# Fused 512-column products for the input projections of a two-layer hybrid decoder

## The chip, the cores and the metric

The kernel runs on one core of one Trainium2 chip. The metric is the device time of one execution in microseconds (us). TensorE is called PE here (its weight loads PEld), VectorE DVE, ScalarE ACT, GpSimd POOL, and SyncE SP; SP issues the loads.

## The reference

Two layers work on one sequence of 256 positions and 2048 features, in fp32. Each layer is `x + RMSNorm_post(mixer(RMSNorm_pre(x)))`.

```python
# layer 0
u = h @ w_in                                # 2048 -> 8192
xr, zr, xm, zm = jnp.split(u, [LRU_WIDTH, 2 * LRU_WIDTH, 2 * LRU_WIDTH + MLSTM_WIDTH], axis=-1)
xr = causal_dwconv(xr, lru_conv_w, lru_conv_b);  yr = rg_lru(xr, ...)
xmc = silu(causal_dwconv(xm, ...));  ym = mlstm_chunkwise(q, k, v, ig, fg) ...
y = concat([yr * silu(zr), ym * silu(zm)]);  return y @ w_out
# layer 1
u = h @ w_in                                # 2048 -> 16384
rkv, z = u[..., :3 * RWKV_WIDTH], u[..., 3 * RWKV_WIDTH:]
rkv = rkv + (shift_right(rkv) - rkv) * mu_rkv;  r, k, v = jnp.split(rkv, 3, axis=-1)
y = rwkv7_scan(rh, wh, kh, vh, kk, ah) ...  ;  return (y * silu(z)) @ w_out
```

`rwkv7_scan` is a recurrence over positions with a 64x64 state for each of 64 heads. The kernel computes it in four chunks of 64 positions, which needs the inverse of a triangular 64x64 matrix for each chunk and head.

## The kernel before

**Precision.** An fp32 product is made of three products of rounded parts. A weight piece `raw` is split into a high part `whi` (a cast on ACT) and a low part `wlo` = raw - whi (a subtraction on DVE), by `split_w`. The normalised input h, features on partitions, positions on columns, is split likewise into `hh` and `hl`. The sum whi x hh + whi x hl + wlo x hh goes to PSUM.

**The input projections** are made by `in_proj`, 512 output features at a time: 16 calls in layer 0 and 32 in layer 1. Layer 1 has eight groups of 512 features (8 heads), each with four calls, in the order k, r, z, v. A call takes 8 pieces, each 256 input features by 512 output features: 512 KB by one DMA of SP, 4 KB in a row, into one of four `raw` buffers (`RAW_BUFS`; three each of `whi` and `wlo`). A piece is 24 matmuls of 256 columns (`in_mms`): 8 of whi x hh alternating with 8 of whi x hl, on the same weights, then 8 of wlo x hh. Two PSUM banks (`gb`, from a pool of four) collect the call's result, and the consumers read it there: the convolutions `conv`, the token shift `shifted` (two operations for each quarter, on ACT and DVE) and the gate `silu2`. For xm, ACT first copies it to SBUF.

**What sets the order.** PE's program order is the order in which matmuls are written (`InOrder` chains them). All other work, such as the recurrences, is written by generators that `Weave` advances: `wv_.tick(dt)` after every few projection matmuls adds dt us to a planned clock, and a generator whose due time has come writes its next step there. DVE and ACT are ordered by a scheduler that ranks instructions by the place where they were written, with `split_w` moved ahead (`high_priority(offset=AHEAD)`). Once built, each engine's order is fixed, and an engine that waits for one instruction holds all those behind it.

**One group of layer 1**, by the names that follow. `keys` forms BK and AR from k. `blocks` has PE multiply them (`mb<-AR,BK 64x64`), and DVE writes the result to `Aab`. `inverse` transposes that to `Ab` and runs 31 dependent steps on DVE (`tf<-Ab,Tb`, then `Tb<-Tb,tf`), then transposes to `TT` and `ZT`; PE then multiplies `ZT,Aab` and `TT,ZT`. In between, `scores` needs the half of `AR` that DVE makes from r (`AR<-rt,Pe`) and has PE multiply `AR,BK 64x128`. `recur` walks the four chunks, each a chain from PE to ACT (`Ws`), PE, DVE (`UV`, two halves of 64 partitions) and PE (`UV,BKt`), while the next group's keys are made. `vt<-gb,vec,vt` is the shift of v, `bi<-Rc,BK` belongs to the value path, `th` to the decay of the next group.

The input tiles of a layer, four of 4 x 128 features, are made on demand by the generator `tiles`, between the first pieces of the layer's first call.

Of the kernel before, what the change touches and what calls it, by code (L numbers as in the profile page):

```python
# [7 lines left out]
F32 = mybir.dt.float32  # L8
F32R = mybir.dt.float32r
# [4 lines left out]
P = 128  # L14
T = 256
# [129 lines left out]
def two_layers(ctx, tc, x, gpost, cst, selc, v0, v1, w_in0, w_out0, w_in1, w_out1, lruw, qkvw,  # L145
# [17 lines left out]
    def gbank():  # L163
        return pg.tile([P, 512], F32, name="gb", tag="gb")

    def mbank():
        return pm.tile([P, 512], F32, name="mb", tag="mb")
# [53 lines left out]
    def in_mms(banks, hi, lo, pc, h, nft, tick):  # L221

        def mm(part, kk, f, hx, first=False, last=False):
            pe.matmul(banks[f // 2][:, (f % 2) * T:(f % 2 + 1) * T], lhsT=part[:, kk, f * P:(f + 1) * P], rhs=hx,
                      start=first, stop=last, skip_group_check=True)

        hs = [tuple(t[:, (2 * pc + kk) % 4, :] for t in h[(2 * pc + kk) // 4]) for kk in range(2)]
# [24 lines left out]
    def half(banks, f):  # L252
        return banks[f // 2][:, (f % 2) * T:(f % 2 + 1) * T]

    def split_y(src, yl):
        yh = hp.tile([P, 4, T], F32R, name="yh", tag="hp")
        act.copy(yh, src)
        dve.tensor_tensor(yl, src, yh.bitcast(F32), SUB)
        return yh, yl

    def out_proj(wsrc, get_y, evac, tick, finish, after, room=None):


# [12 lines left out]
        def piece(c, pc, banks):
            hi, lo = weights(c, pc)
            for part in range(3):
                for kk in range(2):
                    for tt in range(2):  # L280
                        mm(c, pc, hi, lo, part, kk, tt, banks[tt])
                    wv_.tick(tick)

        pair = [[gbank(), gbank()] for _ in range(2)]
        for c in range(2):
            for pc in range(14):
                piece(c, pc, pair[c])
        wv_.drain()
        finish()
        for c in range(2):  # L290
            for pc in range(14, 16):
                piece(c, pc, pair[c])
            evac(c, pair[c])
        for c in range(2, 4):
            banks = [gbank(), gbank()]
# [38 lines left out]
    def to_features(xs, dg, g, warm):  # L334


        banks = {}

        def turn(c, tt):
            if c not in banks:  # L340
                banks[c] = [mbank(), mbank()]
            for f2 in range(2):
                for f in range(2):
                    pe.matmul(banks[c][f2][:, f * T + tt * P:f * T + (tt + 1) * P], lhsT=xs[c][:, tt, (2 * f2 + f) * P:(2 * f2 + f + 1) * P],
                              rhs=dg[tt], start=(tt == 0 and f == 0), stop=True, skip_group_check=True)

        h = []

        def tiles():
            banks[2] = [gbank(), gbank()]  # L350
            keep_warm(warm[0], banks[2][0])
            for c in range(2):
                turn(c, 0)
            keep_warm(warm[1], banks[2][0])
            turn(2, 0)
            for c in range(4):
                if c == 3:
                    turn(c, 0)
                turn(c, 1)
                hh = hp.tile([P, 4, T], F32R, name="hh", tag="hp")  # L360
                hl = hp.tile([P, 4, T], F32R, name="hl", tag="hp")
                for i in range(4):
                    bf = half(banks[c], i)
                    activ(hh[:, i, :], bf, AF.Copy, scale=g(4 * c + i))
                    dve.scalar_tensor_tensor(hl[:, i, :], bf, g(4 * c + i), hh[:, i, :].bitcast(F32), MUL, SUB)
                h.append((hh, hl))
                yield

        grow[0] = tiles()
        next(grow[0])  # L370
        return h
# [20 lines left out]
    def silu2(banks, sz):  # L392

        for b in range(2):
            bk = banks[b].rearrange("p (a t) -> p a t", a=2)
# [24 lines left out]
    with ExitStack() as l0:  # L420
# [230 lines left out]
        def lru(c, yc, lw, res):  # L651
# [24 lines left out]
                                   yc.rearrange("p a t -> p (a t)"), 0.0, MUL, ADD)  # L676
            yield 2.4

        prev = None
        for c in range(4):  # L680
            banks = in_proj(w_in0[(8 + c) * 8:(9 + c) * 8], h)
            wv_.drain(prev)
            xm = t4("xm")
            for b in range(2):
                act.copy(xm[:, 2 * b:2 * b + 2, :], banks[b].rearrange("p (a t) -> p a t", a=2))
            prev = wv_.add(mlstm_in(c, xm))
        wv_.add(gates())
        y0, heads = [], []
        for c in range(4):
            lw = t4("lw")  # L690
            nc.sync.dma_start(lw.rearrange("p a t -> p (a t)"), lruw[:, c, :])
            banks = in_proj(w_in0[c * 8:(c + 1) * 8], h)
            if c == 0:
                wv_.drain(prev)
            yc = t4("yc")
# [6 lines left out]
            banks = in_proj(w_in0[(4 + c) * 8:(5 + c) * 8], h)  # L702
            wv_.drain(g1_)
            sz = t4("sz")
            silu2(banks, sz)
# [1 line left out]
            dve.scalar_tensor_tensor(y, yc, 0.25, sz, MUL, MUL)  # L707
            y0.append(y)
        for c in range(4):
            banks = in_proj(w_in0[(12 + c) * 8:(13 + c) * 8], h)  # L710
            wv_.drain(heads[c])
            sz = t4("sz")
            silu2(banks, sz)
# [28 lines left out]
    with ExitStack() as l1:  # L742
# [38 lines left out]

        def loras():

            banks = [gbank(), gbank()]
# [373 lines left out]
        sts = [{} for _ in range(NG)]  # L1158
        for g in range(NG):
            st = sts[g]  # L1160
            banks = in_proj(w_in1[(8 + g) * 8:(9 + g) * 8], h)
            if g:
                wv_.drain(val[g - 1])
            st["k"] = gt("kt", "kr")
# [20 lines left out]
            banks = in_proj(w_in1[(16 + g) * 8:(17 + g) * 8], h)  # L1185
# [116 lines left out]
```

## Time and profile before

| | |
|---|---|
| time, median of 3 runs | 1917.0 us (1916.63 to 1918.4) |
| the profiled execution | 1918.1 us, span 1916.3 us |
| granted PE clock, mean | 0.995 |
| PE busy | 1890.5 us, 99% |
| DVE busy | 1394.7 us, 73% |
| ACT busy | 1045.2 us, 55% |
| load queue q1 | 45.0% of 16 engines' span |

Lines of a group read: line, engine, operation, output <- inputs, shape, count | busy us, mean ns of one | idle time just before them and what ended it. Lines of the timeline read: start, length, engine, line, operation, with idle time ahead in brackets. L117 and L133 are the lines of the helpers that issue PE's and the other engines' instructions, so tiles tell them apart, not lines. Matmuls overlap, and their mean durations exceed the distance of their starts.

### The profile page before, as it was taken

The page shows a single profiled execution, that of the slowest core. Times are in us where ns is not written, and L with a number is a line of the kernel's source. Part 1 is how long each engine was busy: PE and PEld are TensorE (multiplying, and loading weights), DVE is VectorE, ACT ScalarE, POOL GpSimd, SP SyncE. Part 2 cuts the span into 40 slices and gives each one's busy share as a digit, 9 for nine tenths or more (in the row PEclk, how much of TensorE's full clock was granted, in tenths as well). Part 3 has the DMA queues.
Part 4 walks back from the last instruction along what each step waited for, and adds up shares of the span by engine and source line. Part 5 has one row for each costly group of instructions (what it writes and reads, how often), then busy time and mean ns, then how long its engine had stood idle before and what let it go on. Part 6 is the DMA issues. An engine that isn't in the chain of part 4 may idle for free.

```text
span 1916.3 us, 39538 instructions
## 1 busy us (share of the span) xinstructions
PE 1890.5 (99%) x16506; PEld 1753.2 (91%) x16507; DVE 1394.7 (73%) x2302; ACT 1045.2 (55%) x1609; POOL 59.1 (3%) x84
## 2 busy tenths in 40 slices
PE   9999999999999999999999999999999999999998
PEld 8999999999888899989999999999999999997886
DVE  5667777767555679879689689597796896895544
ACT  6445666645444546555565555655655655555442
POOL 0000000000000000000000000000000000000000
PEclk9999999999999999999999999999999999999999
DMA  7333544445666444423434334344343433356654
GB/s 254 138 133 111 176 165 171 152 173 197 214 202 202 165 144 147 155 106 137 143 130 143 123 130 157 109 150 146 116 147 133 141 133 133 122 186 201 211 202 156
DMA packets 86947, 299.63 MB, mean 156 GB/s; under 512 B 9576, under 2 KB 12392, under 8 KB 86768
## 3 DMA queue, kind: packets, MB, share of 16 engines
q1 hardware_dynamic: 86768, 297.11, 45.0%
q8 instruction: 129, 2.11, 0.4%
q14 instruction: 50, 0.41, 0.1%
HBM read 289.20 MB, written 7.86 MB: 155 GB/s over the span
## 4 chain that ended last, share of the span: by engine, by line
PE 93%; DVE 4%; ACT 1%; issue 1%; DMA 1%; POOL 0%; SPq 0%; DVEq 0%; POOLq 0%; ACTq 0%
PE gb L117 75%; PE mb L117 17%; DVE wlo L133 2%; PE mb L120 1%; ACT whi L133 1%; DVE wb L133 1%; DMA raw<-in_w_in_dram 0%; DVE rt L133 0%; DVE Tb L133 0%; DMA xq<-in_x_dram 0%; DVE tf L133 0%; DVE Ab L133 0%; DVE yT L133 0%; ACT ZT L133 0%; ACT vt L133 0%
## 5 line engine op out<-in xcount | busy, mean ns | idle before, releaser
L133 DVE TENSOR_TENSOR wlo<-raw,whi 128x1024 fp32r<-128x1024 f32 x509 | 619.6, 1218 | 344.2 <-ACT whi L133 308.4
L133 ACT CAST whi<-raw 128x1024 fp32r<-128x1024 f32 x509 | 532.3, 1048 | 553.4 <-PE gb L117 505.1
L117 PE MATMUL gb<-hh,whi 128*128 128x256 f32 x3120 | 793.5, 290 | 2.9 <-ACT whi L133 2.9
L117 PE MATMUL gb<-hl,whi 128*128 128x256 f32 x3120 | 773.7, 284 | 0.5 <-DVE hl L133 0.5
L117 PEld LDWEIGHTS gb<-hh,whi 128*128 128x128 f32 x3120 | 598.8, 192 | 13.6 <-ACT whi L133 3.7
L117 PEld LDWEIGHTS gb<-hl,whi 128*128 128x128 f32 x3120 | 600.0, 192 | 1.9 <-DVE hl L133 1.1
L117 PE MATMUL gb<-hh,wlo 128*128 128x256 f32 x3120 | 454.0, 286 | 0.0
L117 PEld LDWEIGHTS gb<-hh,wlo 128*128 128x128 f32 x3120 | 405.5, 192 | 4.2 <-issue 0.7
L117 PE MATMUL gb<-whi,yl 128*128 128x512 f32 x500 | 136.9, 392 | 0.5 <-DVE yl L133 0.5
L117 PE MATMUL gb<-whi,yh 128*128 128x512 f32 x500 | 136.5, 392 | 0.0
L117 PE MATMUL gb<-wlo,yh 128*128 128x512 f32 x500 | 135.7, 390 | 0.0
L117 PEld LDWEIGHTS gb<-whi,yl 128*128 128x128 f32 x500 | 93.2, 188 | 20.4 <-DVE yl L133 0.9
L117 PEld LDWEIGHTS gb<-wlo,yh 128*128 128x128 f32 x500 | 93.5, 188 | 19.7
L117 PEld LDWEIGHTS gb<-whi,yh 128*128 128x128 f32 x500 | 93.0, 188 | 19.3
L133 DVE TENSOR_TENSOR Tb<-Tb,tf 64x31 f32<-64x31 f32 (+15 forms) x248 | 82.5, 333 | 6.1
L133 DVE TENSOR_TENSOR tf<-Ab,Tb 64x31 f32<-64x31 f32 (+15 forms) x248 | 81.8, 330 | 4.5
L117 PE MATMUL mb<-AR,BK 64*128 64x128 f32 (+1 forms) x1024 | 58.0, 253 | 7.0 <-DVE AR L133 6.0
L117 PEld LDWEIGHTS mb<-AR,BK 64*128 64x128 f32 (+1 forms) x1024 | 50.2, 161 | 13.3 <-PE gb L117 7.1
L133 DVE TENSOR_TENSOR UV<-mb,Gn 64x256 f32<-64x256 f32 x64 | 26.9, 421 | 34.6 <-PE mb L117 33.4
L133 ACT ACTIVATE zz<-kP,dv 128x256 f32<-128x256 f32 x64 | 32.3, 505 | 22.9 <-DVE kP L133 12.4
L117 PEld LDWEIGHTS mb<-UV,At 128*64 128x64 f32 (+1 forms) x1024 | 35.0, 137 | 10.3 <-issue 2.2
L1140 POOL TENSOR_TENSOR vr<-vr,mhalf 128x8 f32<-128x8 f32 x16 | 28.3, 1771 | 505.5 <-DVE vr L133 505.5
(259 smaller groups left out, 1859.7 us busy)
## 6 DMA issues: line engine op xcount, KB each, us to landing
raw<-in_w_in_dram SPq DMA_DIRECT2D x384, 512.0 KB, 3.2
raw<-in_w_out_dram SPq DMA_DIRECT2D x128, 512.0 KB, 4.2
y1d<-zt SPq DMA_DIRECT2D x7, 512.0 KB, 3.5
yraw<-y1d SPq DMA_DIRECT2D x7, 512.0 KB, 3.8
l<-in_lora_dram SPq DMA_DIRECT2D x8, 384.0 KB, 4.3
xq<-in_x_dram SPq DMA_DIRECT2D x8, 256.0 KB, 4.4
lw<-in_lruw_dram SPq DMA_DIRECT2D x4, 512.0 KB, 4.9
xr<-in_x_dram SPq DMA_DIRECT2D x8, 256.0 KB, 6.3
```

Source lines behind the costliest of these rows:

```text
L117: return self._chain(self.eng.matmul(*a, **k))
L120: return self._chain(self.eng.transpose(**k))
L133: r = op(*a, **k)
L1140: pool.tensor_tensor(vr, vr, mhalf[:, 0:8], ALU.pow)
```

## The change

The tiles `hh` and `hl` become one tile `hx`, in which both parts of a feature block stand side by side, 256 + 256 columns. The high weights now multiply these 512 columns in one matmul. The result has two halves for each 128 output features, whi x hh in columns 0 to 255, and whi x hl in columns 256 to 511, to which wlo x hh is added in PSUM. It fills a bank where it filled half of one, so a call makes two turns of 256 output features, each into a pair of banks (the pool holds two pairs, as much as four banks). In a turn a piece is 512 input by 256 output features, as many bytes as before, read by two DMAs of 256 KB, 1 KB in a row. It has 8 matmuls of 512 columns and 8 of 256. After a turn ACT copies the second halves to a new SBUF tile `u`, and DVE adds the first halves to it. The consumers read `u`; the copy for xm is gone. A piece's ticks sum to 2.56 us where they were 2.64, and the four input tiles are asked for in the first four pieces where it was six. Pairs from `gpair` and `gbanks` replace `gbank` elsewhere, with no other effect; the output projections are as they were.

```diff
-    hp = ctx.enter_context(tc.tile_pool(name="hp", bufs=8))
+    hp = ctx.enter_context(tc.tile_pool(name="hp", bufs=4))
-    pg = ctx.enter_context(tc.tile_pool(name="pg", bufs=4, space=PS))
+    pg = ctx.enter_context(tc.tile_pool(name="pg", bufs=2, space=PS))
+    def gpair():
+        return pg.tile([P, 2, 512], F32, name="gb", tag="gb")
...
-    def in_proj(wsrc, h):
-        banks = [gbank(), gbank()]
-        for pc in range(8):
-            w = split_w(load_w(wsrc[pc]))
-            if len(h) < 4 and len(h) <= pc // 2 + 1:
-                next(grow[0])
-            in_mms(banks, *w, pc, h, 4, 0.44)
-        return banks
+    def in_proj(wsrc, h, mk):
+        u = None
+        for j in range(2):
+            t = gpair()
+            for pc in range(4):
+                raw = wp.tile([P, 2, 512], F32, name="raw", tag="raw", bufs=RAW_BUFS)
+                for n in range(2):
+                    src = wsrc[2 * pc + n].rearrange("p (k f) -> p k f", k=2)[:, :, j * 256:(j + 1) * 256]
+                    nc.sync.dma_start(raw[:, n].rearrange("p (k f) -> p k f", k=2), src)
+                hi, lo = (w.rearrange("p n (k f) -> p (n k) f", k=2) for w in split_w(raw))
+                if len(h) < 4 and len(h) <= pc + 1:
+                    next(grow[0])
+                for kk in range(4):
+                    for f in range(2):
+                        pe.matmul(t[:, f, :], lhsT=hi[:, kk, f * P:(f + 1) * P], rhs=h[pc][:, kk].rearrange("p a t -> p (a t)"),
+                                  start=(pc == 0 and kk == 0), stop=False, skip_group_check=True)
+                    wv_.tick(0.42)
+                for kk in range(4):
+                    for f in range(2):
+                        pe.matmul(t[:, f, T:2 * T], lhsT=lo[:, kk, f * P:(f + 1) * P], rhs=h[pc][:, kk, 0, :],
+                                  start=False, stop=(pc == 3 and kk == 3), skip_group_check=True)
+                    if kk % 2:
+                        wv_.tick(0.44)
+            if u is None:
+                u = mk()
+            act.copy(u[:, 2 * j:2 * j + 2, :], t[:, :, T:2 * T])
+            dve.tensor_tensor(u[:, 2 * j:2 * j + 2, :], t[:, :, 0:T], u[:, 2 * j:2 * j + 2, :], ADD)
+        return u
...
-                hh = hp.tile([P, 4, T], F32R, name="hh", tag="hp")
-                hl = hp.tile([P, 4, T], F32R, name="hl", tag="hp")
+                hx = hp.tile([P, 4, 2, T], F32R, name="hx", tag="hp")
...
-            banks = in_proj(w_in0[(8 + c) * 8:(9 + c) * 8], h)
+            xm = in_proj(w_in0[(8 + c) * 8:(9 + c) * 8], h, u0)
             wv_.drain(prev)
-            xm = t4("xm")
-            for b in range(2):
-                act.copy(xm[:, 2 * b:2 * b + 2, :], banks[b].rearrange("p (a t) -> p a t", a=2))
...
-            banks = in_proj(w_in1[g * 8:(g + 1) * 8], h)
+            banks = in_proj(w_in1[g * 8:(g + 1) * 8], h, u1)
```

How this moves instructions is shown at three places of layer 1, all around the fourth group. First PE, at the end of the piece ahead of the product with ZT (x8 are eight products in a row). Before:

```order
L117 MATMUL gb<-hh,whi 128x256
L117 MATMUL gb<-hl,whi 128x256
L117 MATMUL gb<-hh,whi 128x256
L117 MATMUL gb<-hl,whi 128x256
L117 MATMUL gb<-hh,wlo 128x256 x8
L117 MATMUL mb<-ZT,Aab 32x32 x32
L117 MATMUL gb<-hh,whi 128x256
```

and after:

```order
L117 MATMUL gb<-hx,whi 128x512 x8
L117 MATMUL gb<-hx,wlo 128x256 x8
L117 MATMUL gb<-hx,whi 128x512 x8
L117 MATMUL gb<-hx,wlo 128x256 x4
L117 MATMUL mb<-ZT,Aab 32x32 x32
L117 MATMUL gb<-hx,wlo 128x256 x4
L117 MATMUL gb<-hx,whi 128x512 x8
L117 MATMUL mb<-centre,vt 128x128 x8
```

The sixteen alternating products of 256 columns become eight of 512, and the product with ZT now stands in the middle of a piece's low products.

Second, DVE, at the end of the inverse, where the last of its 31 steps lead to the transposes TT and ZT (`u<-gb,u` is the new add, `vt` and `bi` the shift of v and a product of the value path). Before:

```order
L133 TENSOR_TENSOR tf<-Ab,Tb 64x60
L133 TENSOR_TENSOR Tb<-Tb,tf 64x2x30
L133 TENSOR_TENSOR tf<-Ab,Tb 64x31
L133 TENSOR_TENSOR Tb<-Tb,tf 64x31
L133 TENSOR_TENSOR wlo<-raw,whi 128x1024
L133 STREAM_TRANSPOSE TT<-Tb 32x32x32 x2
L133 TENSOR_TENSOR wlo<-raw,whi 128x1024
L133 STREAM_TRANSPOSE ZT<-Tb 32x32x32
L133 TENSOR_TENSOR wlo<-raw,whi 128x1024
L133 TENSOR_TENSOR bi<-Rc,BK 64x1024 x2
```

and after:

```order
L133 TENSOR_TENSOR Tb<-Tb,tf 64x2x30
L133 SCALAR_TENSOR_TENSOR vt<-u,vec_81,vt 128x255
L133 TENSOR_TENSOR tf<-Ab,Tb 64x31
L133 TENSOR_TENSOR wlo<-raw,whi 128x1024
L133 TENSOR_TENSOR Tb<-Tb,tf 64x31
L133 TENSOR_TENSOR bi<-Rc,BK 64x1024
L133 STREAM_TRANSPOSE TT<-Tb 32x32x32
L133 TENSOR_TENSOR wlo<-raw,whi 128x1024
L133 STREAM_TRANSPOSE TT<-Tb 32x32x32
L133 TENSOR_TENSOR wlo<-raw,whi 128x1024
L133 TENSOR_TENSOR u<-gb,u 128x512
L133 STREAM_TRANSPOSE ZT<-Tb 32x32x32
```

An add, a vt, a bi and one more wlo stand in these rows ahead of ZT. From the first Aab of a group to its ZT, DVE has 119 instructions before and 129 after in groups 3 to 7: 5 adds, 2 wlo, 2 vt and 1 bi more. In the first group it is 5 adds and 1 wlo, in the second 4 adds and 1 Sn, and in the last one more (yl) than in the middle ones.

Third, DVE at the update UV of the third chunk (`kP`, `Gn` and `BK` belong to the next group's keys). Before:

```order
L133 TENSOR_SCALAR Gn<-mb 64x8 x4
L133 TENSOR_TENSOR kP<-kt,th 128x1024
L133 RECIPROCAL Gn<-Gn 128x16
L133 TENSOR_TENSOR UV<-mb,Gn 64x4x64 x2
L133 TENSOR_TENSOR BK<-xx,zz 128x4x64
L133 TENSOR_REDUCE vr<-Yn 128x8
```

and after:

```order
L133 TENSOR_SCALAR Gn<-mb 64x8 x4
L133 TENSOR_TENSOR kP<-kt,th 128x1024
L133 RECIPROCAL Gn<-Gn 128x16
L133 TENSOR_TENSOR UV<-mb,Gn 64x4x64
L133 TENSOR_TENSOR wlo<-raw,whi 128x1024
L133 TENSOR_TENSOR BK<-xx,zz 128x4x64
L133 TENSOR_TENSOR UV<-mb,Gn 64x4x64
```

The two halves of UV stood together, and now a wlo and a BK stand between them.

More of the change, by code (lines that the diff above doesn't have):

```diff
@@ L158, in two_layers, with gbanks @@
     sp = ctx.enter_context(tc.tile_pool(name="small", bufs=2))
-    pg = ctx.enter_context(tc.tile_pool(name="pg", bufs=4, space=PS))
+    pg = ctx.enter_context(tc.tile_pool(name="pg", bufs=2, space=PS))
     pm = ctx.enter_context(tc.tile_pool(name="pm", bufs=4, space=PS))
     dr = ctx.enter_context(tc.tile_pool(name="dr", bufs=1, space=bass.MemoryType.DRAM))
-    def gbank():
-        return pg.tile([P, 512], F32, name="gb", tag="gb")
+    def gpair():
+        return pg.tile([P, 2, 512], F32, name="gb", tag="gb")
+    def gbanks():
+        b = gpair()
+        return [b[:, 0], b[:, 1]]
     def mbank():
@@ L225, in mm @@
                       start=first, stop=last, skip_group_check=True)
-        hs = [tuple(t[:, (2 * pc + kk) % 4, :] for t in h[(2 * pc + kk) // 4]) for kk in range(2)]
+        hs = [[h[(2 * pc + kk) // 4][:, (2 * pc + kk) % 4, part, :] for part in range(2)] for kk in range(2)]
         for kk in range(2):
@@ L240, in two_layers @@
     grow = [None]
-    def in_proj(wsrc, h):
-        banks = [gbank(), gbank()]
-        for pc in range(8):
-            w = split_w(load_w(wsrc[pc]))
-            if len(h) < 4 and len(h) <= pc // 2 + 1:
-                next(grow[0])
-            in_mms(banks, *w, pc, h, 4, 0.44)
-        return banks
+    def in_proj(wsrc, h, mk):
[26 more added lines that the diff above has]
+        return u
     def half(banks, f):
+        if not isinstance(banks, list):
+            return banks[:, f, :]
         return banks[f // 2][:, (f % 2) * T:(f % 2 + 1) * T]
+    yhs = []
     def split_y(src, yl):
-        yh = hp.tile([P, 4, T], F32R, name="yh", tag="hp")
+        if not yhs:
+            pair = hp.tile([P, 2, 4, T], F32R, name="yh", tag="hp")
+            yhs.extend([pair[:, 1], pair[:, 0]])
+        yh = yhs.pop()
         act.copy(yh, src)
@@ L282, in piece @@
                     wv_.tick(tick)
-        pair = [[gbank(), gbank()] for _ in range(2)]
+        pair = [gbanks() for _ in range(2)]
         for c in range(2):
@@ L294, in out_proj @@
         for c in range(2, 4):
-            banks = [gbank(), gbank()]
+            banks = gbanks()
             spare = room() if c == 3 and room else []
@@ L349, in tiles @@
         def tiles():
-            banks[2] = [gbank(), gbank()]
+            banks[2] = gbanks()
             keep_warm(warm[0], banks[2][0])
@@ L359, in tiles @@
                 turn(c, 1)
-                hh = hp.tile([P, 4, T], F32R, name="hh", tag="hp")
-                hl = hp.tile([P, 4, T], F32R, name="hl", tag="hp")
+                hx = hp.tile([P, 4, 2, T], F32R, name="hx", tag="hp")
                 for i in range(4):
                     bf = half(banks[c], i)
-                    activ(hh[:, i, :], bf, AF.Copy, scale=g(4 * c + i))
-                    dve.scalar_tensor_tensor(hl[:, i, :], bf, g(4 * c + i), hh[:, i, :].bitcast(F32), MUL, SUB)
-                h.append((hh, hl))
+                    activ(hx[:, i, 0, :], bf, AF.Copy, scale=g(4 * c + i))
+                    dve.scalar_tensor_tensor(hx[:, i, 1, :], bf, g(4 * c + i), hx[:, i, 0, :].bitcast(F32), MUL, SUB)
+                h.append(hx)
                 yield
@@ L394, in silu2 @@
         for b in range(2):
-            bk = banks[b].rearrange("p (a t) -> p a t", a=2)
+            bk = banks[b].rearrange("p (a t) -> p a t", a=2) if isinstance(banks, list) else banks[:, 2 * b:2 * b + 2, :]
             s = sz[:, 2 * b:2 * b + 2, :]
@@ L677, in lru @@
             yield 2.4
+        u0 = lambda: t4("u")
         prev = None
         for c in range(4):
[L681 removed]
+            xm = in_proj(w_in0[(8 + c) * 8:(9 + c) * 8], h, u0)
             wv_.drain(prev)
[L683 to L685 removed]
             prev = wv_.add(mlstm_in(c, xm))
@@ L691, in two_layers @@
             nc.sync.dma_start(lw.rearrange("p a t -> p (a t)"), lruw[:, c, :])
-            banks = in_proj(w_in0[c * 8:(c + 1) * 8], h)
+            banks = in_proj(w_in0[c * 8:(c + 1) * 8], h, u0)
             if c == 0:
@@ L701, in two_layers @@
             heads.append([wv_.add(head(hd)) for hd in (2 * c, 2 * c + 1)][1])
-            banks = in_proj(w_in0[(4 + c) * 8:(5 + c) * 8], h)
+            banks = in_proj(w_in0[(4 + c) * 8:(5 + c) * 8], h, u0)
             wv_.drain(g1_)
@@ L709, in two_layers @@
         for c in range(4):
-            banks = in_proj(w_in0[(12 + c) * 8:(13 + c) * 8], h)
+            banks = in_proj(w_in0[(12 + c) * 8:(13 + c) * 8], h, u0)
             wv_.drain(heads[c])
@@ L782, in loras @@
         def loras():
-            banks = [gbank(), gbank()]
+            banks = gbanks()
             for pc in range(8):
@@ L1145, in two_layers @@
         y1, rec, val, ys_ = {}, {}, {}, {}
+        u1 = lambda: t4("u")
         def final(g, st):
@@ L1160, in two_layers @@
             st = sts[g]
-            banks = in_proj(w_in1[(8 + g) * 8:(9 + g) * 8], h)
+            banks = in_proj(w_in1[(8 + g) * 8:(9 + g) * 8], h, u1)
             if g:
@@ L1176, in two_layers @@
             st["scores"] = wv_.add(scores(g, st), 1)
-            banks = in_proj(w_in1[(24 + g) * 8:(25 + g) * 8], h)
+            banks = in_proj(w_in1[(24 + g) * 8:(25 + g) * 8], h, u1)
             if g:
@@ L1184, in two_layers @@
                 sts[g + 1]["decay"] = wv_.add(decay(g + 1, sts[g + 1]), 3)
-            banks = in_proj(w_in1[(16 + g) * 8:(17 + g) * 8], h)
+            banks = in_proj(w_in1[(16 + g) * 8:(17 + g) * 8], h, u1)
             st["v"] = gt("vt", "vt")
```

## The prediction

> **What bounds the kernel now.** I read the page's shares and chain first, then a table of two stretches, then the waits of PE and DVE, and last the rows of one group of layer 1 in order of time.
>
> ```profile
> span 1916.3 us, 39538 instructions
> PE 1890.5 (99%) x16506; PEld 1753.2 (91%) x16507; DVE 1394.7 (73%) x2302; ACT 1045.2 (55%) x1609; POOL 59.1 (3%) x84
> PE 93%; DVE 4%; ACT 1%; issue 1%; DMA 1%; POOL 0%; SPq 0%; DVEq 0%; POOLq 0%; ACTq 0%
> L117 PE MATMUL gb<-hh,whi 128*128 128x256 f32 x3120 | 793.5, 290 | 2.9 <-ACT whi L133 2.9
> ```
>
> PE is busy 99% of the span and carries 93% of the chain that ended last: the kernel is a queue of matmuls, and whatever shortens that queue shortens the time, as long as nobody else becomes late. The 3120 products are 48 of the loras and 3072 = 384 pieces x 8 of the input projections. The next question is how much air the others have, and that differs by stage:
>
> ```profile
> 0.00:652.00 652.00, 647.12 (x4463) 594.23 (x4465) 418.37 (x664) 345.36 (x488) 12.26 (x34) 1.00 0.52 177
> 980.00:1113.00 133.00, 131.66 (x1395) 125.54 (x1391) 106.96 (x184) 76.22 (x127) 5.62 (x6) 0.99 0.39 135
> ```
>
> The columns are stretch, length, then busy time of PE, PEld, DVE, ACT, POOL, the granted clock and the DMA share. In layer 0 (first row) DVE is busy 418.37 of 652 us, 64%; in one group of layer 1 (second row) 106.96 of 133, 80%. An average of 80% hides where the 20% lies. The rows of that group, DVE and PE mixed, show it:
>
> ```profile
> 980.69 2.30 PE L117 MATMUL mb<-AR,BK 64*64 64x64 f32 x64
> 981.83 0.43 DVE L133 TENSOR_TENSOR BK<-xx,zz 128x256 f32<-128x256 f32 x1 [1.89 <-ACT zz L133]
> 982.29 1.39 DVE L133 TENSOR_TENSOR Aab<-mb,Gn 64x512 f32<-64x512 f32 x2
> 1000.38 1.16 PE L117 MATMUL mb<-AR,BK 64*128 64x128 f32 x16 [1.00 <-DVE AR L133]
> 1036.79 0.69 DVE L133 TENSOR_SCALAR th<-th 128x1024 f32<-128x1024 f32 x1 [1.08 <-ACT th L133]
> 1051.10 2.23 DVE L133 STREAM_TRANSPOSE ZT<-Tb 32x1024 f32<-32x1024 f32 x1
> 1054.87 2.21 PE L117 MATMUL mb<-ZT,Aab 32*32 32x32 f32 x64
> ```
>
> Brackets give an idle time ahead of the row. From the first Aab (982.29) to the end of ZT (1051.10 + 2.23 = 1053.33) DVE has one wait, 1.08 us, in 71.0 us: this window is DVE's own length. It opens after a real wait of DVE (1.89), so its start hangs on PE and ACT, not on an older backlog. PE needs its last product, ZT, at 1054.87: DVE is 1.54 us early. In the middle, at AR, DVE is already late by 1.00. The table of waits says the same for all groups:
>
> ```profile
> PE mb L117 <- DVE AR L133: 6.0, 6, 1.0
> ```
>
> Six groups, 1.0 us each. So PE bounds the kernel everywhere, and DVE is within 1.5 us of bounding it in a 71 us window of each group.
>
> **Part 1, what the fused product saves.** Starts, not durations, give a matmul's price, since they overlap:
>
> ```profile
> 701.62 1.12 PE L117 MATMUL gb<-hh,wlo 128*128 128x256 f32 x8
> 702.58 0.28 PE L117 MATMUL gb<-hh,whi 128*128 128x256 f32 x1
> ...
> 520.01 1.07 PE L117 MATMUL gb<-whi,yh 128*128 128x512 f32 x4
> 520.92 1.07 PE L117 MATMUL gb<-whi,yl 128*128 128x512 f32 x4
> 521.82 1.07 PE L117 MATMUL gb<-wlo,yh 128*128 128x512 f32 x4
> 522.73 0.84 PE L117 MATMUL gb<-whi,yh 128*128 128x512 f32 x3
> ```
>
> Eight of 256 columns take 702.58 - 701.62 = 0.96 us, 120 ns each. Twelve of 512 columns, in the output projection, take 522.73 - 520.01 = 2.72 us, 226.7 ns each. A pair of 256 becomes one of 512: 240 - 226.7 = 13.3 ns saved, 8 pairs a piece, 0.106 us a piece (24 x 0.120 = 2.88 becomes 2.77). Over 384 pieces that is 40.9 us: 13.6 in layer 0 (128 pieces), 27.2 in layer 1 (256 pieces, 3.41 a group of 32).
>
> The Trainium skill, "TensorE: Matmul & The Clock Gate", section "Back-to-back issue gap", puts the fixed part of an isolated product at 2.5 ns, by which the fusion would save 2.5 x 3072 = 7.7 us (an estimate) and the sum below would be 33 us higher. The rows have 120 and 226.7, so the fixed part here is 13.3, and I keep it.
>
> **Part 2, what it adds on ACT and DVE.** Each of the 48 projections now leaves PSUM in two turns: one ACT copy and one DVE add of 128x512 each, 96 of both, and the 8 xm copies go. Rows of the nearest kind:
>
> ```profile
> L133 ACT COPY xm<-gb 128x512 f32<-128x512 f32 x8 | 4.6, 590 | 0.0
> L133 DVE TENSOR_TENSOR vt<-vt,mb 128x512 f32<-128x512 f32 x16 | 10.2, 677 | 0.1
> 1003.73 0.67 DVE L133 TENSOR_TENSOR At<-mb,cs 128x512 f32<-128x512 f32 x1
> 1004.33 0.30 DVE L133 TENSOR_TENSOR Tb<-Tb,tf 64x156 f32<-64x156 f32 x1
> ```
>
> ACT: 88 x 0.59 = 52 us on an engine at 55%, costed at nothing; its cover is the time of a turn, 4 x 2.77 = 11.1 us, before the pair of banks is wanted again, against 0.59 + 0.68 for copy and add. That cover holds with a DVE up to 9 us late. DVE: 96 adds; one of this shape, reading PSUM, holds DVE 1004.33 - 1003.73 = 0.60 us. In layer 0, with DVE at 64%, I cost them at nothing.
>
> Consumers that read PSUM now read SBUF. The same operation on the same shape from both:
>
> ```profile
> L133 DVE SCALAR_TENSOR_TENSOR zt<-zt,gb 128x512 f32<-128x512 f32 x16 | 10.1, 671 | 0.0
> L133 DVE SCALAR_TENSOR_TENSOR zt<-yT,zt 128x512 f32<-128x512 f32 x16 | 10.9, 683 | 0.1
> ```
>
> 671 and 683 ns: nothing either way.
>
> **Part 3, loads.** A piece comes as two transfers of 256 KB in runs of 1 KB instead of one of 512 KB:
>
> ```profile
> q1 hardware_dynamic: 86768, 297.11, 45.0%
> raw<-in_w_in_dram SPq DMA_DIRECT2D x384, 512.0 KB, 3.2
> raw<-in_lora_dram SPq DMA_DIRECT2D x8, 192.0 KB, 2.8
> ```
>
> No row has 1 KB runs. The nearest is the loras' load, 192 KB in runs of 768 bytes, as many runs (256) as one new transfer has: 2.8 us to land, against 3.2 for the whole old piece. Bounds: nothing, if both halves travel together; 5.6 us a piece if one after the other, still inside the 11 us that four raw buffers give a piece, but a queue that never overlapped would then need 5.6 us for each 2.77 of PE. Queue use of 45% speaks for overlap. I take nothing; SP's added issues, 384, have no one waiting on that queue in between but the same loads.
>
> **Part 4, the window of layer 1.** Counted in the changed order, the stretch of DVE from Aab to ZT in the middle groups holds ten instructions more: 5 of the new adds, 2 more wlo, 2 vt and 1 bi, the last five pulled ahead of ZT from behind it. Their starts:
>
> ```profile
> 1005.16 1.20 DVE L133 TENSOR_TENSOR wlo<-raw,whi 128x1024 fp32r<-128x1024 f32 x1
> 1006.29 0.32 DVE L133 TENSOR_TENSOR tf<-Ab,Tb 64x175 f32<-64x175 f32 x1
> ...
> 1054.33 2.44 DVE L133 TENSOR_TENSOR bi<-Rc,BK 64x1024 f32<-64x1024 f32 x2
> 1056.80 1.23 DVE L133 TENSOR_TENSOR wlo<-raw,whi 128x1024 fp32r<-128x1024 f32 x1
> 1057.94 0.87 DVE L133 SCALAR_TENSOR_TENSOR vt<-gb,vec,vt 128x255 f32<-128x255 f32 x2
> 1058.73 0.48 DVE L133 SCALAR_TENSOR_TENSOR bl<-bi,vec,bh 128x256 fp32r<-128x256 f32 x1
> ```
>
> wlo 1.13, bi 2.47 / 2 = 1.24, vt 0.79 / 2 = 0.395. Sum: 5 x 0.60 + 2 x 1.13 + 2 x 0.395 + 1.24 = 7.29 us. I let it fill the one wait of 1.08, so ZT ends 6.21 later: before, 1053.33 - 980.69 = 72.64 after the blocks; now 78.85. Without waits PE would want ZT at 74.18 (1054.87 - 980.69) less the 1.00 at AR less its own saving in this stretch. That stretch held 496 products of 0.120 and now holds 172 of 0.120 and 168 of 0.2267: 59.52 becomes 58.73, 0.79 saved. So 72.39, and PE waits 78.85 - 72.39 = 6.5 us, some of it at AR, the rest at ZT.
>
> A second place is the update UV in the group's third chunk, between whose two halves the new order puts one wlo and one BK:
>
> ```profile
> 966.47 0.88 DVE L133 TENSOR_TENSOR UV<-mb,Gn 64x256 f32<-64x256 f32 x2
> 967.04 1.04 PE L117 MATMUL mb<-UV,BKt 128*64 128x64 f32 x16
> 967.38 0.43 DVE L133 TENSOR_TENSOR BK<-xx,zz 128x256 f32<-128x256 f32 x1
> 967.72 0.68 DVE L133 TENSOR_REDUCE vr<-Yn 128x8 f32<-128x512 f32 x1
> ```
>
> 1.13 + 0.34 = 1.47 us later at most, nothing at least; PE starts right behind the first half, so I stay near the upper end, 1.2.
>
> Per group: 78.85 - 74.18 = +4.67 in the window, -(3.41 - 0.79) = -2.62 outside it, +1.2 at UV: +3.25. I take six groups so (2 to 7): +19.5. The first two have shorter lists (+4.1 and +2.8 us of DVE), about their own saving of 3.41: 0.
>
> **Part 5, starts.** All four input tiles are wanted within a layer's first four pieces rather than six. Not in the trace; between 0 and the 2.9 us that PE lost to whi in all (the gb row above), for each layer. I take 1 each: +2.
>
> **Sum.** -13.6 + 19.5 + 2 = +7.9 us. The profiled execution took 1918.1 (span 1916.3), 1.1 above the median, so it becomes 1926.0 and the median 1924.9, 0.4% slower. A change of 0.2%, 3.8 us, is about what the runs can tell from none.
>
> **Rivals.**
> A, faster: the five pulled instructions (2 wlo, 2 vt, bi: 4.29 us) cost the window nothing, because they only fill waits that DVE will have there. The price is 6 x 4.29 = 25.7: 1924.9 - 25.7 = 1899. For it: DVE is idle 26 us of each group; against: only 1.08 of them lie in the window. The sum turns at 7.9 / 6 = 1.3 of the 4.29.
> B, full saving: DVE's lateness never reaches PE. 1917.0 - 40.9 + 2 = 1878. Against: 1.54 us of room for 6.2.
> C, stalls and saving cancel: 1917, if the stall is 5.2 rather than 6.5 a group.
> D, the lateness also reaches the other three chunks' UV, 1.2 each: +3.6 x 6 = 21.6, 1946. Against: only one has a wlo moved between its halves.
> E, the fused product saves nothing in this stage (240 ns): 1966. Against: 226.7 in twelve neighbouring rows of the output projection.
>
> **How the numbers follow.** Forecast 0.43, A 0.22, C 0.18, B 0.09, D 0.06, E 0.02. The forecast's own range is 1916 (1.2 and the starts at nothing) to 1937 (the 1.08 not filled, UV 1.47, starts 2.9 each); most of it is over 0.2% slow. With D and E slower comes to 0.51, A and B make faster 0.31, C same 0.18. The range goes from A with a few us below it, 1895, to 1940; outside stay B, D and E, 0.17.
>
> **What would show it.** Right: 3072 products gb<-hx,whi of 512 columns, starts 227 ns apart; layer 0 about 13 us shorter; in the waits of PE, AR and ZT together near 6.5 us a group and UV near 1.2; 78.9 us from the blocks to the product with ZT where 74.2 were. Wrong: waits of PE from DVE near 1 us a group as now (B), or ZT on time and only AR late (A); waits of gb for raw or whi (loads); starts 240 apart (E).

## The result, and the profile after

The changed kernel takes 2012.4 us (median of 4 runs, 2009.4 to 2017.5) against 1916.8 for the kernel before: a ratio of 1.050, interval 1.049 to 1.052. It is 5% slower. The prediction had the sign and 1925; its range ended at 1940. The profiled execution took 2009.4, span 2007.6, so the trace has to explain 2007.6 - 1916.3 = 91.3 us.

The page of the changed kernel: span, busy shares, the chain that ended last, and the groups of the fused product and of the new add.

```profile
span 2007.6 us, 34549 instructions
PE 1910.4 (95%) x13435; PEld 1614.4 (80%) x13435; DVE 1450.3 (72%) x2398; ACT 1096.1 (55%) x1697; POOL 56.5 (3%) x84
PE 85%; DVE 10%; ACT 2%; issue 1%; DMA 1%; POOL 0%; SPq 0%; DVEq 0%; POOLq 0%; ACTq 0%
L117 PE MATMUL gb<-hx,whi 128*128 128x512 f32 (+1 forms) x3168 | 844.6, 404 | 5.8 <-ACT whi L133 3.8
L133 DVE TENSOR_TENSOR u<-gb,u 128x512 f32<-128x512 f32 x96 | 65.6, 684 | 0.6
```

PE is busy 95% where it was 99%, and DVE carries 10% of the chain where it had 4%. DVE's own share of the span did not rise (72%, 73 before), so an average over the span would have cleared it.

What PE waited for, in all (total, times, longest):

```profile
PE mb L117 <- DVE AR L133: 29.0, 6, 4.9
PE mb L117 <- DVE ZT L133: 13.6, 7, 2.2
PE mb L117 <- DVE UV L133: 13.4, 7, 2.0
PE mb L120 <- DVE yn L133: 7.2, 3, 5.0
PE mb L117 <- DMA l<-in_lora_dram: 3.7, 1, 3.7
```

And the mean granted clock of PE, of the changed kernel and of the kernel before:

```profile
core 0: 2007.6 us, clock 0.964
...
core 0: 1916.3 us, clock 0.995
```

3.6% of 2007.6 is 72 us of clock that PE was not given, 10 before. Most of that loss lies right behind the waits. In the third group (PE and DVE mixed, idle time in brackets):

```profile
1005.89 2.08 PE L117 MATMUL mb<-AR,BK 64*64 64x64 f32 x64
1007.09 2.10 DVE L133 TENSOR_TENSOR Aab<-mb,Gn 64x512 f32<-64x512 f32 x3 [2.17 <-PE mb L117]
1012.76 0.69 DVE L133 TENSOR_TENSOR Yn<-Yn,vr 128x512 f32<-128x512 f32 x1 [1.04 <-POOL vr L1170]
1028.29 2.08 PE L117 MATMUL mb<-AR,BK 64*128 64x128 f32 x16 [4.83 <-DVE AR L133]
1085.23 2.02 DVE L133 STREAM_TRANSPOSE ZT<-Tb 32x1024 f32<-32x1024 f32 x1
1087.30 3.36 PE L117 MATMUL mb<-ZT,Aab 32*32 32x32 f32 x64 [1.92 <-DVE ZT L133]
```

PE stands at AR for 4.83 us and at ZT for 1.92: 6.75, where the prediction had 6.5. PE now takes ZT 0.05 us after DVE is done with it, where it had 1.54 us in hand. Two stretches right behind these waits (length, busy times, granted clock):

```profile
1028.30:1033.10 4.80, 4.80 (x27) 4.38 (x28) 3.93 (x11) 1.63 (x2) 0.13 (x1) 0.50 0.32 105
1087.30:1094.10 6.80, 6.80 (x74) 6.23 (x75) 5.24 (x8) 2.86 (x6) 0.00 (x0) 0.53 0.34 111
```

PE is busy all the time, at half its clock. The trace has 27 such stretches, of 3.4 us or a multiple (the last of a trace is cut by its end); before it had six. Not all need a wait. In the kernel before, four of the six stand behind the products with ZT and TT, two times 64 small products, where PE waited 0.30 us (length, busy times, granted clock):

```profile
1059.80:1063.20 3.40, 3.10 (x72) 2.85 (x72) 3.34 (x7) 3.34 (x6) 0.00 (x0) 1.00 0.64 248
1063.20:1066.60 3.40, 3.40 (x18) 3.40 (x18) 0.39 (x1) 1.25 (x2) 0.00 (x0) 0.50 0.47 160
```

Set against each other stage by stage (starts of the first product of each stage, in the two profiled executions; the 14.7 and 15.1 us ahead of the first projection are left out):

| stage | before, us | after | difference |
|---|---|---|---|
| layer 0, to the first projection of layer 1 | 637.6 | 639.8 | +2.2 |
| start of layer 1, to the first group's blocks | 80.0 | 87.1 | +7.0 |
| eight windows, blocks to ZT,Aab | 594.8 | 652.7 | +57.9 |
| the stretches behind the windows, to the next blocks or the output projection | 383.0 | 398.1 | +15.0 |
| last output projection, to the end | 206.1 | 214.9 | +8.7 |

The last output projection starts 3.6 us (before) and 6.9 us (after) ahead of the last group's product with ZT, so the fourth row counts the last of its stretches as negative. The last row holds that group's wait for ZT (1.72) and the longest stretch of half clock (10.2 us).

### The profile page after: what moved, and what is told of

The parts are those of the page before. It is cut to its first block, busy times and chain, and to the rows that moved or that the text cites. A ratio compares the mean times of both kernels' runs of the same rounds, so it can differ in the third digit from the quotient of the medians.

```text
span 2007.6 us, 34549 instructions
## 1 busy us (share of the span) xinstructions
PE 1910.4 (95%) x13435; PEld 1614.4 (80%) x13435; DVE 1450.3 (72%) x2398; ACT 1096.1 (55%) x1697; POOL 56.5 (3%) x84
## 3 DMA queue, kind: packets, MB, share of 16 engines
q8 instruction: 105, 1.72, 0.3%
## 4 chain that ended last, share of the span: by engine, by line
PE 85%; DVE 10%; ACT 2%; issue 1%; DMA 1%; POOL 0%; SPq 0%; DVEq 0%; POOLq 0%; ACTq 0%
PE gb L117 68%; PE mb L117 16%; DVE wlo L133 3%; PE mb L120 2%; DVE Ab L133 1%; ACT whi L133 1%; DVE ZT L133 1%; DMA raw<-in_w_in_dram 1%; DVE rt L133 1%; DVE u L133 1%; DVE wb L133 1%; DVE tf L133 0%; DMA l<-in_lora_dram 0%; POOL vr L1170 0%; DVE hx L133 0%
## 5 line engine op out<-in xcount | busy, mean ns | idle before, releaser
L117 PE MATMUL gb<-hx,whi 128*128 128x512 f32 (+1 forms) x3168 | 844.6, 404 | 5.8 <-ACT whi L133 3.8
L117 PEld LDWEIGHTS gb<-hx,whi 128*128 128x128 f32 x3168 | 574.4, 195 | 112.6 <-ACT whi L133 5.1
L117 PE MATMUL gb<-hx,wlo 128*128 128x256 f32 x3120 | 467.5, 289 | 0.0
L117 PEld LDWEIGHTS gb<-hx,wlo 128*128 128x128 f32 x3120 | 435.4, 193 | 33.2 <-issue 1.0
L117 PE MATMUL mb<-AR,BK 64*128 64x128 f32 (+1 forms) x1024 | 63.8, 273 | 34.9 <-DVE AR L133 29.0
L117 PEld LDWEIGHTS mb<-AR,BK 64*128 64x128 f32 (+1 forms) x1024 | 54.9, 179 | 43.9 <-issue 33.8
L133 DVE TENSOR_TENSOR u<-gb,u 128x512 f32<-128x512 f32 x96 | 65.6, 684 | 0.6
L133 ACT COPY u<-gb 128x512 f32<-128x512 f32 x96 | 55.9, 583 | 5.5 <-PE gb L117 5.0
L133 DVE TENSOR_TENSOR At<-mb,cs 128x512 f32<-128x512 f32 x64 | 41.9, 678 | 4.5 <-PE mb L117 4.4
```

The costliest lines, as they stand in the source:

```text
L117: return self._chain(self.eng.matmul(*a, **k))
L133: r = op(*a, **k)
```

## The experiments

Times are medians, each beside runs of the kernel before on the same chip; that kernel's median was 1915.2 to 1916.9 in all of them.

**What the half clock costs.** Fillers in three waits:

```diff
                 ab = [mbank(), mbank()]
+                if f == 0 and g >= 2:
+                    keep_warm(22, ab[0])
...
             zb = [mbank(), mbank()]
+            keep_warm(9, zb[0])
...
+                    if c == 2 and g < NG - 1:
+                        keep_warm(9, sb)
```

> The changed kernel with bf16 filler products of 512 columns written ahead of three products in layer 1 that wait for DVE: 22 ahead of a group's first AR,BK 64x128 (groups 3 to 8), 9 ahead of ZT,Aab and 9 ahead of UV,BKt of the third chunk. Each lasts about 216 ns at full clock, so they fill the waits of 4.8, 1.9 and 2.0 us and lengthen nothing that DVE sets. Theory 1 (each wait of PE is paid twice: once as idle time, and again because PE gets half its clock for 3.4 to 6.8 us afterwards, 57 us in all over before): the waits stay, the half-clock stretches of these places go, time near 1962 us. Rival (the clock's loss lies in time that DVE would hold anyway): no gain, 2005 to 2015 us, although the granted clock rises.

Measured: 1989.2 us, ratio 1.038 (1.037 to 1.040), between the two expectations. PE of this kernel at the third group's AR, and the stretch behind:

```profile
1027.70 4.92 PE L117 MATMUL mb<-ones 128*128 128x512 bf16 x21
1032.60 1.16 PE L117 MATMUL mb<-AR,BK 64*128 64x128 f32 x16
...
1032.60:1037.40 4.80, 4.80 (x39) 4.17 (x38) 4.53 (x15) 2.19 (x3) 0.13 (x1) 1.00 0.30 100
```

The waits are filled, the clock behind them is 1.00, and it is 0.985 over the span. One stretch of half clock stays in each middle group, ahead of UV, where PE has small products and no wait. The time falls by 23 us, not by 50 (the two profiled executions lie 16.7 apart). The middle groups' windows stay at 81.1 us (81.4), since DVE sets their length however fast PE is; the gain is all between the windows (59 us a group where it was 60 to 62) and at the end. So both theories hold, each in its place: half clock is paid where PE is the bound, and free where DVE is.

**Is it the fused product at all?** Its undoing, with turns, loads, copy and add kept:

```diff
-                        pe.matmul(t[:, f, :], lhsT=hi[...], rhs=h[pc][:, kk].rearrange("p a t -> p (a t)"), ...)
+                        for a in range(2):
+                            pe.matmul(t[:, f, a * T:(a + 1) * T], lhsT=hi[...], rhs=h[pc][:, kk, a, :], ...)
```

> The changed kernel with the fusion undone and all else kept: two turns of 256 features, loads of 256 KB, copy and add to u, but each 512-column product written as two of 256 columns. Theory 1 (the stalls come from the DVE work in the window, not from PE having become faster): PE loses the 38 us saved, the stalls at AR, ZT and UV stay within 2 to 3 us of 8.7 a group (one add and one wlo leave the window in the built order, 1.7 us), time 2010 to 2040 us, slower than before by 5% as well. Rival (the faster PE runs into a DVE that is as fast as before): the stalls go back to about 1 us a group and the time to 1920 to 1935 us.

Measured: 1999.5 us, 1.044 (1.042 to 1.045): below the expected band, and 13 us faster than the fused form. The middle windows are 80 to 81 us, and AR is waited for nearly as long as in the changed kernel (29.0):

```profile
PE mb L117 <- DVE AR L133: 26.5, 6, 4.5
```

With PE's saving given back most of the loss stays: it belongs to the turns with their loads, copy and add, and a faster PE only waits more. Layer 0's projections, where DVE has room, do show the fused product: 460.8 us in pairs, 452.8 fused, 8.0 us.

**The adds alone.** In layer 1:

```diff
-            dve.tensor_tensor(u[...], t[:, :, 0:T], u[...], ADD)
+            act.copy(ua[...], t[:, :, 0:T])
+            pool.tensor_tensor(u[...], ua[...], u[...], ADD)
```

> The changed kernel with the adds of layer 1 taken off DVE: ACT copies both halves to SBUF and POOL adds them; layer 0 unchanged. In the built order a group's window on DVE has exactly the five adds less (125 instructions for 130, 120 before), the pulled wlo, vt and bi stay. Theory 1 (window is DVE's length, each us of it is a us of stall, and each stall over some 2 us brings 3.4 to 6.8 us at half clock): stalls at AR plus ZT fall from 6.7 to about 3.7 us a group, UV stays at 2, some half-clock stretches go: 1970 to 1990 us. Rival (the pulled instructions and the new order do it, the adds are innocent): 2000 us or more. A third outcome, below 1930 us, would say that the adds were nearly all of it.

Measured: 2000.9 us, 1.045 (1.043 to 1.047): the rival's number, but not for its reason. Five adds left DVE, and the windows stayed at 81 to 82 us. DVE's rows beside POOL's, in this kernel, and the same DVE row in the changed one:

```profile
1024.90 2.38 DVE L133 TENSOR_TENSOR yT<-yT,vt 128x512 f32<-128x512 f32 x2
...
1024.27 1.86 POOL L281 TENSOR_TENSOR u<-u 128x512 f32<-128x512 f32 x1 [6.82 <-ACT u L133]
```

```profile
1020.16 1.29 DVE L133 TENSOR_TENSOR yT<-yT,vt 128x512 f32<-128x512 f32 x2
```

While POOL adds, DVE's two yT take 2.38 us, not 1.29. Summed over the fourth group's window without DVE's waits, DVE's time is 77.5 us for 125 instructions and 76.3 for 130. Beside four of POOL's five adds in it one DVE instruction takes 1.0 to 1.1 us more than in the changed kernel, 4.1 us in all, where the five adds were worth 3.0. The adds came back as slower DVE work, so this run does not tell the adds from the pulled instructions.

**Less and more DVE work in the window.** Half of the low weights left out in layer 1:

```diff
-            dve.tensor_tensor(lo[:, :, 0:w], raw[:, :, 0:w], ...)
+            dve.tensor_tensor(lo[:, 0:n, 0:w], raw[:, 0:n, 0:w], ...)      # n = 1 in layer 1's projections
...
-                        pe.matmul(t[:, f, T:2 * T], lhsT=lo[:, kk, ...], ...)
+                        pe.matmul(t[:, f, T:2 * T], lhsT=lo[:, kk % 2, ...], ...)
```

> The changed kernel with half of the low weights left out in layer 1: DVE subtracts only the first 256 of a piece's 512 input features, and both halves of the low products use that half. PE's work is the same. In the built order the window holds 128 instructions (one add and one wlo fewer), 19 of them wlo at about 0.57 us less: some 12 us less DVE in it. Theory 1 (window is DVE's length, and DVE is the whole loss in layer 1): blocks to ZT,Aab falls from 81.3 to PE's own 72 to 73 us, stalls at ZT 0, at AR under 2 (its chain from the projection through copy, add and shift stays), time 1915 to 1935 us. Rival (copy, add and shift form a chain that is late by its latency): AR's stall stays near 4.8, time 1960 us or more.

Measured: 1918.0 us, 1.0005 (0.999 to 1.002), as theory 1 had it. The third group on PE, and what is left of PE's waits for scores:

```profile
989.84 2.08 PE L117 MATMUL mb<-AR,BK 64*64 64x64 f32 x64
1064.22 1.95 PE L117 MATMUL mb<-ZT,Aab 32*32 32x32 f32 x56
...
PE mb L117 <- DVE At L133: 8.6, 13, 1.9
```

74.4 us for the window, no wait for AR or ZT. A middle group takes 129.3 us where the kernel before took 132.6. That this is about the forecast saving of 3.41 is chance: most groups of the kernel before hold a stretch of half clock, worth 1.7 us. Groups without one are 131.1 before and 129.3 here, 1.8 us apart, and the AR wait of 1.0 that went is in that. The eight windows and the stretches behind them are together 12.8 us shorter than before; the start of layer 1 (+4.8) and the last output projection (+6.7) give most of that back, layer 0 and its start the rest. The same from the other side, in the kernel before:

```diff
+            s = scr_[0]()
+            for b in (0, 1, 0, 1):
+                dve.tensor_tensor(s[:, 2 * b:2 * b + 2, :], banks[b]..., h[b][0]..., ADD)
```

> The kernel before with four more DVE adds of 128x512 from PSUM after each projection of layer 1, their results unused: exactly eight more instructions (4.8 us) in each group's window in the built order, and nothing else there. PE's order and loads are as before. Theory 1 (DVE work in the window beyond 1.5 us of room becomes PE's waiting and then half clock): blocks to ZT,Aab 2 to 4 us longer than 74.2, waits at AR 2 to 4 us, and 1940 to 1960 us. Rival (before had room for it, and the loss belongs to the new order of PE): within 8 us of before.

Measured: 2020.3 us, 1.054 (1.052 to 1.056): the direction of theory 1, and more than twice its size. PE's two largest waits:

```profile
PE mb L117 <- DVE AR L133: 26.1, 6, 4.4
PE mb L117 <- ACT sq L133: 15.1, 19, 1.3
```

Sixteen unused adds a group, eight of them (4.8 us) in its window, cost 103 us: 5 to 6 us in each middle window, 5 to 7 behind it (where sq is waited for), 10 at the start of layer 1, with half clock behind most of the waits. The kernel before stands at an edge, without any fused product.

**Asking later.** One due time moved:

```diff
-            yield 1.8
+            yield 8.8
             yield 1
             Amm = Aab.rearrange("p f h c i -> p (f h c) i")
```

> The changed kernel with one planned time moved: the step of the inverse that multiplies by ZT is due 7 us later. In the built order of groups 4 to 7 PE's products AR,BK 64x128 then stand 20.4 us of projection work behind the blocks (14.3 in the changed kernel) and ZT,Aab 66.6 us (58.7); group 3 has only ZT later, group 8 only AR. DVE has as much to do. Theory 1 (DVE is not short of time over a group, 112 of 143 us; PE asks too early in its window): the waits at AR and ZT of these groups go, and with them the half clock after them, 9 to 10 us a group, 1965 to 1975 us. Rival (a group is bound by DVE's length however PE's products are placed): the waits move to other products of the same groups, 2005 us or more.

Measured: 1952.4 us, 1.018 (1.016 to 1.020): 60 us less, more than expected. In the fourth group neither product has a wait:

```profile
1175.64 1.16 PE L117 MATMUL mb<-AR,BK 64*128 64x128 f32 x16
...
1237.76 2.21 PE L117 MATMUL mb<-ZT,Aab 32*32 32x32 f32 x64
```

That group takes 130.5 us, less than before (132.7, with a stretch of half clock in it), with all of DVE's added work in it. In the third group, where only ZT moved, AR still waits 4.8 us. DVE is not too slow for a group; PE asked too early inside it.

**The change in layer 0 alone**, layer 1 with the projection of the kernel before:

> The change made in layer 0 alone; layer 1 has the projection of the kernel before. Theory 1 (all of the loss but the last steps of layer 0 comes from layer 1): layer 1 as before, layer 0 as in the changed kernel (453 us for its projections where it was 453, 187 where it was 184 after them), 1915 to 1922 us. Rival (a general cost of the change, such as loads in 1 KB runs or a slower clock over all): 1930 us or more.

Measured: 1945.1 us, 1.015 (1.013 to 1.016): the rival's side, and a miss. Layer 0 came as expected (451 and 187 us). The rest is 6 us at the start of layer 1, 18 us in the eight groups, 0.4 to 4 each, and 2 us behind them. At the start of layer 1 PE waits for the second weights of the loras (`l`), as it does in the changed kernel, though layer 1's pieces are whole here; the load landed 0.2 us before this product:

```profile
711.32 3.51 PE L117 MATMUL mb<-hid,l 96*128 96x256 f32 x8 [3.90 <-issue]
```

What is new in the groups is a wait at a product that has the same place on PE as before:

```profile
PE mb L117 <- ACT sq L133: 10.2, 8, 1.4
```

It is 1.3 to 1.4 us in seven of the groups, with a stretch of half clock behind each. On ACT, ahead of the third group, the last of the four sq stands behind the copies to Ws and Yn, which it stood ahead of before. That they move because banks are now taken in pairs is a guess; it was not tried apart.

**Two smaller places.** Layer 0's ticks (planned times), then the load of the loras' second weights:

```diff
-                    wv_.tick(0.42)
+                    wv_.tick(0.43 if mk is u0_[0] else 0.42)      # and 0.46 for 0.44
```

> The changed kernel with the planned time of a piece in layer 0 put back from 2.56 to 2.64 (ticks of 0.43 and 0.46). In the built order the last head's product vtok,Dt then stands 6.0 us of projection work ahead of the layer's last projection product, as before (6.7); in the changed kernel it stands behind it, and its transpose yn follows at once with a wait of 5.0 us. Theory (layer 0 lost its saving because ten planned microseconds fewer push the last head past the end of the projections): the wait and the half clock behind it go, 7 to 11 us less, 2001 to 2005 us. Rival (layer 0's saving is eaten by the new adds and copies themselves): no change, 2009 us or more.

Measured: 2000.7 us, 1.044 (1.042 to 1.046). The median has the expected drop, but its runs spread from 1997 to 2009, and its trace (2008.9) doesn't show it: the last head's wait of 5.0 is gone, a wait of 3.15 stands at an earlier yn, and layer 0 is only 2 us shorter. Inconclusive.

```diff
+                st["l2"] = t4("l2", (2, 512))[0:96]
+                nc.sync.dma_start(st["l2"], lora2[:, 0, :, :])
                 loras()
```

> The changed kernel with one load moved: the loras' second weights of the first group are asked for ahead of the loras' own pieces, not after them. In the changed kernel SP issues this load behind 13 half-piece loads (6.5 pieces), each of which waits for a free buffer; before it stood behind 5 pieces. PE waits 3.7 us for it and then has half clock for 6.8 us. Theory (the wait is a place in SP's queue, and is paid twice): 6 to 8 us less, 2004 to 2006 us. Rival (PE would wait for something else there, and the clock falls anyway): 2009 us or more.

Measured: 2003.7 us, 1.046 (1.044 to 1.047), 8.7 less. The start of layer 1 is back at 80.3 us (87.1 after, 80.0 before).

**All retimings together**, then two further sets of due times:

> The changed kernel with its planned times adapted: the product with ZT 7 us later in groups 2 to 7 (2.5 in the first, none in the last), the scores of group 3 6 us later, layer 0's ticks at 2.64, the first load of the loras' second weights ahead. Nothing is computed otherwise. From the 1952 us with ZT moved alone: AR of group 3 (4.8 us and its clock) 8 less, the last group's wait for yl (8.0 and its clock) 11 less, layer 0 some 9, the lora load 7. Theory (with PE asking later, DVE's added work fits beside PE and the fused product's 38 us show): 1910 to 1925 us, thus about the time of before, since the first two groups and UV still wait. Rival (DVE's added work finds the next place to hold PE up): 1940 us or more.

> The retimed kernel (1933 us) with four planned times more: layer 0's transposes yn 1.6 us later, the step of values 1.3 us later, ZT 1 us earlier in group 2 and 4 us later in the last group. Aimed at its largest waits: yn 3.2 and 1.2, vt 7.2 over five groups, ZT 3.9 in the last group, At 3.0 in group 2, each with a stretch of half clock. Theory (each wait is a due time that no longer fits, and is paid up to twice): 10 to 18 us less, 1915 to 1923 us. Rival (DVE's added work finds the next place): 1930 us or more.

> As the run above, with larger steps (yn 3.1 us later, values 2 us later) and ZT only 1 us later in the first group and 3 us in the last. In the built order two of the middle groups hold four more DVE instructions in the window and their scores come 0.5 us sooner or later in turns. Theory: 1912 to 1925 us. Rival: 1930 us or more. A difference between the two runs shows what a microsecond of planned time does.

Measured: 1933.2 us, 1.008 (1.007 to 1.010); then 1931.1 (1.009, 1.007 to 1.010) and 1953.6 (1.021, 1.018 to 1.023). Groups 3 to 7 take 128.9 to 133.3 us in the first and 126.9 to 130.4 in the second (131.1 to 132.7 before), but no run beats the kernel before. Largest waits of the first:

```profile
PE mb L117 <- DVE vt L133: 7.2, 5, 3.1
PE mb L117 <- DVE UV L133: 6.1, 6, 1.8
```

The second removed the vt wait and got a wait of 7.6 us for yl in the last group; the third, with due times 0.7 to 1.5 us apart from the second's, lost 22 us to half clock and small waits. The first run lies between its theory (1925 at most) and its rival (1940 or more); in the other two the rival held. Moved by hand, DVE's added work does find the next place.

## Why the prediction was wrong

The forecast's terms beside the trace, from the profiled execution before:

| stage | forecast, us | measured |
|---|---|---|
| ahead of layer 0's projections (the start) | +1 | +0.3 |
| layer 0 | -13.6 | +2.2 |
| start of layer 1 | +1 | +7.0 |
| the eight windows | 6 x 4.67 = +28.0 | +57.9 |
| behind the windows (with UV) | 6 x -1.42 = -8.5 | +15.0 |
| last output projection | 0 | +8.7 |
| sum (differences rounded) | +7.9 | +91.3 |

**The window: right in its mechanism, wrong in its length.** DVE as the setter of the window and AR and ZT as the places came out, and 6.5 us of waiting a group did too (6.75). But the window grew by 7.2 us, not 4.67. The added work was smaller than its term: 6.3 us, from 70.0 to 76.3 in the fourth group, DVE's waits left out, against 7.29. The step that failed is "I let it fill the one wait of 1.08, so ZT ends 6.21 later": in that group ZT ends 8.95 later behind the first Aab, since DVE's waits grew from 1.08 to 3.75. In the third group they are:

```profile
DVE Yn L133 <- POOL vr L1170: 1.0, 1, 1.0
DVE wlo L133 <- PE gb L117: 1.0, 1, 1.0
DVE th L133 <- ACT th L133: 0.9, 1, 0.9
DVE wlo L133 <- ACT BKt L133: 0.5, 1, 0.5
DVE At L133 <- PE mb L117: 0.4, 1, 0.4
```

Only 1.4 of them end by PE. With the clock held up by the fillers they still come to 3.4, so half clock is not what makes most of them; what does was not tried apart.

That the stall of 6.5 came out is luck in part. In the third group DVE ended ZT 81.36 us after the blocks (1087.25 - 1005.89), not 78.85, and PE without its waits would have come after 81.42 - 6.75 = 74.67, not 72.39. The two errors, 2.5 and 2.3, nearly cancel. A clock of 0.50 in the 4.80 us behind AR would explain most of PE's error: half of that, 2.4 us, as an estimate.

**What lies behind a wait had no term.** The sum counted idle time only. Behind most of the waits came 3.4 to 6.8 us at half clock. Filling three of the waits gave 23 us back. The stretches between windows, forecast at -1.4 a group, became +1.8 to +5.4 behind groups 2 to 7; with the fillers they are +0.3 to +1.9 behind groups 3 to 7. Before, five stretches of half clock stood in the groups already, four of them behind the products with ZT and TT, and I gave them no price. The Trainium skill, "TensorE: Matmul & The Clock Gate", section "What's actually happening", has half clock as the state after an idle window of about 3.4 us, and a busy window as what ends it; the trace's stretches of 3.4 and 6.8 us agree, but here waits of 1.3 to 2 us beside small products were enough, and in the kernel before two times 64 small products with 0.30 us between.

**The first two groups at nothing.** "About their own saving" was wrong: +7.1 and +7.1 in their windows, like the rest, and -3.2 and +4.6 behind them. DVE's added work in the window is a delay, and at most the first group got a saving of PE elsewhere to set against it.

**Loads: hidden, but a queue was not.** The two half loads landed in 3.2 us as the whole piece did, and no wait of PE is put down to raw. But "no one waiting on that queue in between but the same loads" was false. SP before, then after, and the product that waits:

```profile
686.67 13.29 SPq L218 DMA_DIRECT2D raw<-in_w_in_dram  x5
700.01 0.42 SPq L823 DMA_DIRECT2D l<-in_lora_dram  x1
```

```profile
690.32 16.13 SPq L257 DMA_DIRECT2D raw<-in_w_in_dram  x13
706.49 0.59 SPq L853 DMA_DIRECT2D l<-in_lora_dram  x1
...
713.25 3.75 PE L117 MATMUL mb<-hid,l 96*128 96x256 f32 x8 [3.69 <-DMA l<-in_lora_dram]
```

The loras' load now stands behind 6.5 pieces, each of which waits for a free buffer, where it stood behind 5. Moved ahead, 8.7 us came back: the wait and the clock behind it. Halving the loads is not needed for that: with the change in layer 0 alone it stands behind seven whole pieces, and PE waits 3.90 us. What moves it was not tried.

**The fused product: 10 ns, not 13.3.** Its starts in the changed kernel:

```profile
1018.20 2.00 PE L117 MATMUL gb<-hx,whi 128*128 128x512 f32 x8
1020.04 1.11 PE L117 MATMUL gb<-hx,wlo 128*128 128x256 f32 x8
```

1.84 / 8 = 230 ns, where the output projection's rows gave 226.7. So 31 us rather than 40.9, 10 of them in layer 0. There it showed 8.0 against the same kernel in pairs, but the turns around it cost 7.4, and with 2.8 us more behind the projections -13.6 became +2.2. "I cost them at nothing" failed there in small places: a last head of yn with a wait of 5.0, two of 0.9 and 1.3, half clock behind them. How much is due to the ten planned microseconds fewer stays open.

**The rivals.** D had the direction (the lateness reaches further places) but not the place: it was the first two groups, the start and the end. A, B and C fell with the first window, and E with the starts 230 ns apart. UV waited 1.7 to 2.0 rather than 1.2.

## What to carry to other kernels

Price a saving on the busiest engine together with what it hangs on the engine that is nearly as busy, in the stretch where that one runs without a gap: there 6 us of added work gave 7 us, while the average showed room. Then price every new wait of PE twice, as idle time and as a stretch of half clock wherever PE is the bound. And where an order is written from planned times, a cheaper step moves everything that was timed against it: put the consumer's due time later (one number gave 60 of the 95.6 us back) before giving the idea up, and look at what stands behind more loads in an issuing queue.

## What the runs showed of the hardware

- Half clock followed waits of PE as short as 1.3 to 2 us (sq 1.38, UV 1.91, ZT 1.92) where products around them were small, and two times 64 products of 32x32 with a wait of 0.30 between, in stretches of 3.4 us or a multiple; with bf16 fillers in the waits for AR and ZT the clock behind them was 1.00.
- 64 POOL adds of 128x512 in SBUF took 1.35 us in the median (1.27 to 5.48); beside one of 1.86 us DVE's two adds took 2.38 us, not 1.29.
- The 512-column product of the projections starts every 230 ns, that of the output projection every 227; why was not tried.
